# The MLP's second product by seven block products instead of eight, in a two-layer encoder on one core

## The chip, the core and the metric

The kernel runs on one core of a Trainium2 chip. The core has a matrix engine (TensorE, in the profile PE, its weight loads PEld), three engines for elementwise work (VectorE is DVE, ScalarE is ACT, GpSimd is POOL) and SyncE (SP), whose queue issues the loads here. Each engine works through its own list of instructions in order and waits on semaphores for the others. Matrix products read on-chip memory (SBUF) and write into PSUM, of which there are eight banks of 128 x 512 float32. The metric is the device time of one execution in microseconds, as the median of several runs; lower is better.

## The reference

Two layers over 256 tokens of 2048 features, float32. Each layer normalises, projects into three groups of attention heads, sends their outputs through an output projection, and ends in an MLP with 8192 hidden features:

```python
x = x + jnp.einsum('bse,ed->bsd', mix, w_o[l])
h = rmsnorm(x, norm_mlp[l])
u = jax.nn.relu(jnp.einsum('bsd,df->bsf', h, w_up[l]))      # (256, 2048) x (2048, 8192)
x = x + jnp.einsum('bsf,fd->bsd', u * u, w_down[l])          # (256, 8192) x (8192, 2048)
```

A final norm follows the second layer. The two MLP products read 134 MB of weights per layer, each weight once.

## The kernel before

**Three passes for one product.** Every dense product is made in float32 accuracy from a narrower matmul format: an operand a is split into hi (a cast, on ACT) and lo = a - hi (a subtraction, on DVE), and the matmuls hi x hi, hi x lo and lo x hi are added up in PSUM. Activations are split once; each weight tile is split after its load.

**Tiles and steps.** The program is a list of steps, one per weight tile of 128 x 1024 float32 (512 KB): two blocks of 128 rows by 512 columns. For each step `load` (L770) issues the DMA into one of six `wraw` buffers, seven steps ahead; `split` (L776) makes `whi` (L783, ACT) and `wlo` (L784, DVE), two steps ahead, in four buffers each; then the step's `mm` records its matmuls. After each step a queue of background pieces (attention, transposes) may add some PE work; in the MLP there is none. The instructions' order on each engine comes from a scheduler that runs over what the Python code records.

**First product of the MLP** (`up_steps`, L592). Weights are the stationary operand, so features come out on partitions and the 256 tokens on columns. A chunk of 512 features takes two banks and 8 steps of 24 matmuls with 256 columns (L611 to L613). Then for each bank: ReLU on ACT (L617), the square on POOL (L618), hi on ACT (L621), lo on DVE (L622). The norm's factor is left out here, as it passes through ReLU and square as its square.

**Second product** (`down_steps`, L626). For a group g of 1024 hidden features and a chunk j of 512 output columns, 4 steps of 12 matmuls with 512 columns (`mode_b`, L446 to L448) fill two banks, one per block of 128 tokens. DVE then adds each bank, times the squared norm factor, into the residual x (L643). The first product's chunks of group g + 1 are recorded ahead of the second product of group g.

The buffers the change touches: 24 general ones of 4 KB per partition (`big`), 6 of 2 KB (`mid`), six PSUM banks for products and transposes, and two more (`S`) for attention scores.

Of the kernel before, what the change touches and what calls it, by code (L numbers as in the profile page):

```python
# [17 lines left out]
F32 = mybir.dt.float32  # L18
# [5 lines left out]
P = 128  # L24
# [10 lines left out]
# mixer feature blocks of 256 (two k-blocks each): A 0-1, B 2-3, C 4-7  # L35
# [8 lines left out]
def tile_trunk(ctx: ExitStack, tc: tile.TileContext, x_in, w_in, w_o, w_up, w_down,  # L44
# [19 lines left out]
    def big(dt, *shape):  # L64
        return dp.tile([P, *shape], dt, tag="big", bufs=24, name=nm("big"))

    def mid(dt, *shape):
        return dp.tile([P, *shape], dt, tag="mid", bufs=6, name=nm("mid"))
# [4 lines left out]
    def mm_bank():  # L73
        return pp.tile([P, 512], F32, tag="bank", bufs=6, name=nm("mm"))

    def tr_bank():
        return pp.tile([P, 512], F32, tag="bank", bufs=6, name=nm("tr"))

# [10 lines left out]
    ones = cp.tile([P, 64], F32, name="ones")  # L89
# [16 lines left out]
    def setup_tables():  # L106
        """Rope tables with the gains folded in: out = x * ctab + swap16(x) * stab."""
# [14 lines left out]
    def setup_avec():  # L122
        """Relative-position vector of group A, reversed: avec[h, i] = bias(h, rel = 255 - i)."""
# [3 lines left out]
        oh = dp.tile([33, 512], F32, tag="mid", bufs=6, name="oh")  # L127
        nc.sync.dma_start(oh, onehot)
        avs = dp.tile([8, 512], F32, tag="mid", bufs=6, name="avs")
# [30 lines left out]
    def tick():  # L160
        cur[0] += 2.6
# [16 lines left out]
    def hprep(key, gcol, j, hT, ss, done, fin_rs, late=0):  # L178
        """Column chunk j of x: partial sums of squares; k-blocks 4j..4j+3 of the operand."""
# [59 lines left out]
    def q_transposes(src, pr0, qT):  # L239
        """src [P, t, heads*64]; 4 heads from pair pr0 -> qT [hi;lo, 4, 256]."""  # L240
# [13 lines left out]
    def k_transposes(src, pr0, npr, kh, kl):  # L254
        """src [P, t, heads*64]; head pairs pr0.. -> hi/lo [every head in both halves, heads, 256]."""
# [13 lines left out]
    def v_split(ps, parts, t, r):  # L269
        """Value columns of one bank, scaled, as hi/lo; parts: (first column, heads, tile)."""  # L270
# [7 lines left out]
    def rope(raw, H, which, l, outs):  # L278
        """raw [P, t, H, 64]: per-head RMS norm, gain and axial rotary, in place of outs(t)."""
# [29 lines left out]
    def queue_unit(u, *preps):  # L309
        """Scores, transposes of the weights, product with the values; spaced for the softmax between."""  # L310
# [6 lines left out]
    def unit_scores(u):  # L317
        S = pp.tile([P, 4, 256], F32, tag="S", bufs=1, name=nm("S"))
        for s in range(4):
            qh, kh, qb = u.slot(s)  # L320
            st = u.qT[:, qh, qb * P:(qb + 1) * P]
            nc.tensor.matmul(S[:, s, :], st, u.kh[:, kh, :], start=True, stop=False)  # L322
            nc.tensor.matmul(S[:, s, :], st, u.kl[:, kh, :], start=False, stop=True)  # L323
# [4 lines left out]
        if u.kind == "C":  # L328
            nc.vector.tensor_reduce(negm, S, axis=AX.X, op=ALU.max, negate=True)
            src = S  # L330
        else:
            for b in range(2):
                nc.vector.scalar_tensor_tensor(p[:, 2 * b:2 * b + 2, :], S[:, 2 * b:2 * b + 2, :], 0.125,
# [7 lines left out]
            src = p  # L341
# [601 lines left out]
```

## Time and profile before

| | |
|---|---|
| runs | median 2088.99 us of 3 (2088.61 to 2090.86) |
| profiled execution | span 2088.3 us from its first to its last instruction; granted TensorE clock 0.997 on the mean |
| instructions | 31322 |
| loads | 381.49 MB, 183 GB/s on the mean |

The three runs lie within 0.1% of each other, and the span of the profiled execution is 0.7 us below their median. The page gives busy times of each engine, the chain of work that ended last, and groups of instructions by line. In a group's row, the two numbers behind the first bar are its busy time in us and the mean of one instruction in ns; behind the second bar stands how long the engine was idle just ahead of them and what ended that. `128x1024 f32` is partitions by elements. In a timeline's row the first number is the start and the second the duration, both in us. In a table of stretches each engine has its busy time and, in brackets, its instructions, in the order PE, PEld, DVE, ACT, POOL; then come the granted clock (1.00 is full), the busy share of the DMA queues and GB/s. Matmuls overlap each other in PE's pipeline, so the mean of one (0.389 us for 512 columns) is longer than the distance from one to the next.

### The profile page before, as it was taken

What the parts mean: (1) busy time and instruction counts of PE and PEld (TensorE: products, weight loads), DVE (VectorE), ACT (ScalarE), POOL (GpSimd) and SP (SyncE); (2) the same over time, 40 slices, a digit from 0 to 9 for tenths busy, and PEclk for the clock granted to TensorE, in tenths of its full rate; (3) what the DMA queues carried; (4) which work ended last, traced back from release to release, by engine and by line L of the source; (5) the groups of instructions that cost most, each with busy time, mean ns of one, the idle gap of its engine ahead of it and who ended that gap; (6) DMA issues with size and microseconds to landing.
All of it is one profiled execution on the core that took longest, in us unless ns stands there. A gap on an engine that the chain in (4) does not pass through costs nothing.

```text
span 2088.3 us, 31322 instructions
## 1 busy us (share of the span) xinstructions
PE 2066.0 (99%) x12444; PEld 1847.9 (88%) x12444; DVE 1273.8 (61%) x1426; ACT 1041.4 (50%) x1472; POOL 340.1 (16%) x362
## 2 busy tenths in 40 slices
PE   9999999999999999999999999999999999999998
PEld 7878889989899898998888788899899898999986
DVE  6777976454555545555668789754555545555555
ACT  6657755444344444434556566554344444434444
POOL 0484420000000000000005844101000000000001
PEclk9999999999999999999999999999999999999999
DMA  8545455565655656556556453555655656565563
GB/s 289 179 160 157 155 185 176 183 192 180 194 186 187 192 183 192 187 188 189 188 177 188 141 170 130 180 174 181 194 188 183 192 189 191 184 192 185 190 212 121
DMA packets 107550, 381.49 MB, mean 183 GB/s; under 512 B 11875, under 2 KB 14691, under 8 KB 107404
## 3 DMA queue, kind: packets, MB, share of 16 engines
q1 hardware_dynamic: 107116, 378.45, 56.6%
q8 instruction: 97, 1.59, 0.3%
q10 hardware_dynamic: 288, 1.05, 0.1%
q14 instruction: 49, 0.40, 0.1%
HBM read 377.34 MB, written 2.11 MB: 182 GB/s over the span
## 4 chain that ended last, share of the span: by engine, by line
PE 94%; POOL 2%; DVE 1%; ACT 1%; issue 1%; DMA 0%; SPq 0%; POOLq 0%; DVEq 0%
PE mm L446 18%; PE mm L447 18%; PE mm L448 18%; PE mm L612 12%; PE mm L613 12%; PE mm L611 12%; PE tr L362 1%; PE tr L192 1%; PE tr L381 1%; PE S L323 1%; PE S L322 1%; POOL big L300 1%; POOL big L506 0%; PE tr L245 0%; POOL sm L235 0%
## 5 line engine op out<-in xcount | busy, mean ns | idle before, releaser
L784 DVE TENSOR_TENSOR wlo<-wraw,whi 128x1024 fp32r<-128x1024 f32 (+1 forms) x697 | 863.4, 1241 | 697.4 <-ACT whi L783 695.0
L783 ACT CAST whi<-wraw 128x1024 fp32r<-128x1024 f32 (+1 forms) x697 | 729.9, 1048 | 884.6 <-PE mm L448 473.0
L446 PE MATMUL mm<-whi,big 128*128 128x512 f32 (+1 forms) x1792 | 695.7, 389 | 3.1 <-DVE big L252 3.1
L447 PE MATMUL mm<-wlo,big 128*128 128x512 f32 (+1 forms) x1792 | 693.0, 387 | 0.0
L448 PE MATMUL mm<-whi,big 128*128 128x512 f32 (+1 forms) x1792 | 692.4, 386 | 0.0
L611 PE MATMUL mm<-big,whi 128*128 128x256 f32 x2048 | 579.8, 283 | 0.0
L613 PE MATMUL mm<-big,wlo 128*128 128x256 f32 x2048 | 579.6, 283 | 0.0
L612 PE MATMUL mm<-big,whi 128*128 128x256 f32 x2048 | 579.6, 283 | 0.0
L446 PEld LDWEIGHTS mm<-whi,big 128*128 128x128 f32 x1792 | 337.8, 189 | 68.1 <-issue 3.4
L448 PEld LDWEIGHTS mm<-whi,big 128*128 128x128 f32 x1792 | 337.4, 188 | 68.0
L447 PEld LDWEIGHTS mm<-wlo,big 128*128 128x128 f32 x1792 | 337.9, 189 | 64.8 <-DVE wlo L784 0.2
L612 PEld LDWEIGHTS mm<-big,whi 128*128 128x128 f32 x2048 | 393.2, 192 | 0.5
L611 PEld LDWEIGHTS mm<-big,whi 128*128 128x128 f32 x2048 | 393.1, 192 | 0.5
L613 PEld LDWEIGHTS mm<-big,wlo 128*128 128x128 f32 x2048 | 393.1, 192 | 0.0
L618 POOL TENSOR_TENSOR mid<-mid 128x512 f32<-128x512 f32 x64 | 74.2, 1159 | 1247.3 <-ACT mid L617 1247.3
L353 POOL TENSOR_SCALAR big<-big,sm 128x256 f32<-128x256 f32 x128 | 87.5, 701 | 230.3 <-DVE sm L351 164.3
L643 DVE SCALAR_TENSOR_TENSOR x<-mm,sm,x 128x512 f32<-128x512 f32 x128 | 89.9, 744 | 4.5 <-PE mm L448 4.5
L622 DVE TENSOR_TENSOR big<-mid,big 128x512 fp32r<-128x512 f32 x64 | 44.1, 689 | 50.7 <-ACT big L621 50.7
L621 ACT CAST big<-mid 128x512 fp32r<-128x512 f32 x64 | 39.8, 621 | 50.7 <-POOL mid L618 50.7
L617 ACT ACTIVATE mid<-mm,zero 128x512 f32<-128x512 f32 x64 | 43.8, 684 | 39.5 <-PE mm L613 39.5
L235 POOL TENSOR_TENSOR sm<-sm,mhalf 128x2 f32<-128x2 f32 (+3 forms) x16 | 24.7, 1547 | 131.0 <-DVE sm L230 117.0
L364 DVE TENSOR_TENSOR big<-tr,big 128x512 fp32r<-128x512 f32 x64 | 41.1, 680 | 0.3
(117 smaller groups left out, 1013.2 us busy)
## 6 DMA issues: line engine op xcount, KB each, us to landing
wraw<-in_w_up_dram SPq DMA_DIRECT2D x256, 512.0 KB, 4.3
wraw<-in_w_down_dram SPq DMA_DIRECT2D x256, 512.0 KB, 4.1
wraw<-in_w_in_dram SPq DMA_DIRECT2D x120, 512.0 KB, 3.3
wraw<-in_w_o_dram SPq DMA_DIRECT2D x64, 512.0 KB, 3.6
biasB<-in_rpb_dram SPq DMA_DIRECT2D x16, 349.5 KB, 6.2
biasA<-avec SPq DMA_DIRECT2D x4, 768.0 KB, 4.9
x<-in_x_dram SPq DMA_DIRECT2D x3, 512.0 KB, 9.1
big<-in_gfin_dram SPq DMA_DIRECT2D x2, 512.0 KB, 4.3
```

Source lines behind the costliest of these rows:

```text
L353: nc.gpsimd.tensor_scalar(p[:, s, :], p[:, s, :], rs[:, s:s + 1], 1.0, op0=ALU.mult, op1=ALU.mult)
L446: nc.tensor.matmul(o, a_h, wh[:, i, :], start=first and i == 0, stop=False)
L447: nc.tensor.matmul(o, a_h, wl[:, i, :], start=False, stop=False)
L448: nc.tensor.matmul(o, a_l, wh[:, i, :], start=False, stop=last and i == len(sub) - 1)
L611: nc.tensor.matmul(o, sh, ht[:, 0, kk, :], start=s0, stop=False, skip_group_check=True)
L612: nc.tensor.matmul(o, sh, ht[:, 1, kk, :], start=False, stop=False, skip_group_check=True)
L613: nc.tensor.matmul(o, sl, ht[:, 0, kk, :], start=False, stop=s1, skip_group_check=True)
L618: nc.gpsimd.tensor_mul(a, a, a)
L622: nc.vector.tensor_sub(uf[:, 1, :], a, f(uf[:, 0, :]))
L643: nc.vector.scalar_tensor_tensor(xs, box["b"][t], st["r2"][:, t:t + 1], xs, op0=ALU.mult, op1=ALU.add)
L783: last_hi[0] = nc.scalar.copy(h[:, part], w[:, part]).ins
L784: nc.vector.tensor_sub(lo[:, part], w[:, part], f(h[:, part]))
```

## The change

**Seven products.** The second product is cut into quads: 1024 hidden features by 1024 output columns (group g, half n). In a quad, tokens are halved (two blocks of 128), output columns are halved (two of 512), and the features of each step are two blocks of 128. That is a 2 x 2 by 2 x 2 block product, and the Winograd form of Strassen's algorithm makes it with 7 products of sums instead of 8 products. The sums of activation blocks and of weight blocks are made on POOL, the hi/lo split is made of the sums, and the 7 products are summed over the quad's 4 steps in 7 banks. At its end the banks are combined into the four blocks of x, by ACT, DVE and POOL (`down_evac`). The last half of the last group (g = 7, n = 1) stays a plain product (`down_last`, 8 steps of 12 matmuls).

**Activations.** The first product is made in units of 256 features with one bank: 4 steps of 24 matmuls with 256 columns. Since sums of two token blocks need the tokens' factors in them, the squared norm factor now goes into the activations: a row of 256 factors is laid out over all partitions once per layer (`st["rr"]`, made with two matmuls), and POOL multiplies by it. `F` holds eight blocks of 128 columns: the four of the unit and four sums.

**Weights.** A quad step has two tiles, ra and rb. POOL makes four differences of 512 columns (`forms`, one of them in place in ra); what is split then are ra, rb and three half tiles in `T`: 7 blocks of 512 columns for 4. `whi` and `wlo` share ten buffers, of which a quad step takes eight.

**Order.** A pair of quad steps and a unit of the first product follow each other: in each group 0 to 6, pair, unit, four times over, the two quads of the group one after the other. The last quad's four steps stand together.

**Else.** Attention scores take two banks of a common set of eight. `big` has 22 buffers, `mid` 7.

```diff
+        def up_unit(q):
...
+                    for kk in range(4):
+                        ht, hk = st["hT2"][2 * k + kk // 2], kk % 2
+                        for fs in range(2):
+                            o = box["b"][:, fs * 256:(fs + 1) * 256]
...
+                    if k == 3:
+                        up_evac(q, box["b"])
+                return Step([w_up[l, q * 4 + k]], 4, 256, pre, mm, 2.9)
+        def up_evac(q, bank):
+            need(("rr", l))
+            a = mid(F32, 512)
+            nc.scalar.activation(a, bank, AF.Relu, bias=zero1[:, 0:1])
+            nc.scalar.activation(a, a, AF.Square, bias=zero1[:, 0:1])
+            F = big(F32, 8, P)
+            av = a.rearrange("p (k t c) -> p t k c", k=2, t=2)
+            rv = st["rr"].rearrange("p (t o c) -> p t o c", t=2, o=1)
+            for t in range(NT):
+                s0 = 2 - 2 * t
+                nc.gpsimd.tensor_mul(F[:, s0:s0 + 2, :], av[:, t], rv[:, t].to_broadcast([P, 2, P]))
+            nc.gpsimd.tensor_add(F[:, 4, :], F[:, 0, :], F[:, 1, :])
+            nc.gpsimd.tensor_sub(F[:, 5, :], F[:, 2, :], F[:, 0, :])
+            nc.gpsimd.tensor_sub(F[:, 6, :], F[:, 4, :], F[:, 2, :])
+            nc.gpsimd.tensor_sub(F[:, 7, :], F[:, 3, :], F[:, 6, :])
+            c0 = 0 if q >= 28 else 1
+            Fh, Fl = big(F32R, 8, P), big(F32R, 8, P)
+            nc.scalar.copy(Fh[:, c0:8, :], F[:, c0:8, :])
+            nc.vector.tensor_sub(Fl[:, c0:8, :], F[:, c0:8, :], f(Fh[:, c0:8, :]))
+            uT[q] = (Fh, Fl)
+        PRODUCTS = ((2, 0, 0), (4, 2, 0), (3, 1, 1), (7, 1, 0), (6, 2, 1), (5, 0, 1), (1, 3, 0))
+        def down_quads(g, n):
...
+                    Fh, Fl = uT[4 * g + p]
+                    for o, (a, part, i) in zip(box["b"], PRODUCTS):
+                        bh, bl = w[part][0][:, i, :], w[part][1][:, i, :]
+                        nc.tensor.matmul(o, Fh[:, a, :], bh, start=p == 0, stop=False)
+                        nc.tensor.matmul(o, Fh[:, a, :], bl, start=False, stop=False)
+                        nc.tensor.matmul(o, Fl[:, a, :], bh, start=False, stop=p == 3)
+                    if p == 3:
+                        down_evac(n, box["b"])
...
+        def down_evac(n, banks):
...
+            nc.scalar.copy(s1, p1)
+            nc.scalar.copy(s5, p5)
+            nc.vector.tensor_add(x11, x11, p2)
+            nc.vector.tensor_add(x12, x12, p3)
+            nc.vector.tensor_add(u2, s1, p6)
+            nc.vector.tensor_add(u3, u2, p7)
+            nc.vector.tensor_sub(x21, x21, p4)
+            nc.gpsimd.tensor_add(x11, x11, s1)
+            nc.gpsimd.tensor_add(col2, col2, one(s5))
+            nc.gpsimd.tensor_add(x12, x12, u2)
+            nc.gpsimd.tensor_add(row1, row1, one(u3))
...
+        steps.extend(alternate(up_unit(0), up_unit(1)) + up_unit(2) + up_unit(3))
         for g in range(8):
-            if g < 7:
-                up_steps(g + 1)
-            down_steps(g)
+            down = down_quads(g, 0) + (down_quads(g, 1) if g < 7 else down_last(1))
+            per = len(down) // 4
+            for i in range(4):
+                if g == 7:
+                    steps.extend(down[:4] if i == 0 else down[4:] if i == 1 else [])
+                    continue
+                steps.extend(down[per * i:per * i + per])
+                steps.extend(up_unit(4 * (g + 1) + i))
...
+    def part(w, first=False):
+        k, n = w.shape[1:]
+        h = wp.tile([P, k, n], F32R, tag="whl", bufs=10, name=nm("whi"))
+        lo = wp.tile([P, k, n], F32R, tag="whl", bufs=10, name=nm("wlo"))
...
+        if s.forms:
+            ra, rb = raw
+            T = sp.tile([P, 3, 512], F32, tag="bias", bufs=2, name=nm("forms"))
+            nc.gpsimd.tensor_sub(T[:, 0, :], ra[:, 1, :], ra[:, 0, :])
+            nc.gpsimd.tensor_sub(ra[:, 1, :], rb[:, 0, :], ra[:, 1, :])
+            nc.gpsimd.tensor_sub(T[:, 1, :], rb[:, 0, :], T[:, 0, :])
+            nc.gpsimd.tensor_sub(T[:, 2, :], T[:, 1, :], rb[:, 1, :])
+            parts_t[i] = [part(ra), part(rb), part(T[:, 0:2, :]), part(T[:, 2:3, :])]
+            return
```

What the change does to the lists of POOL and ACT shows best in their order. POOL before, at the seam from attention to the MLP (L408 to L417 are the last sums of squares of attention, L618 the squares of the first product; from there on the list holds only L618 to the layer's end):

```order
L408 TENSOR_TENSOR mid_595_2993<-mid_578_2900 128x512
L417 TENSOR_TENSOR sqacc_557_2795<-sqacc_557_2795,mid_595_2993 128x256 x2
L235 TENSOR_TENSOR sm_609_3058<-sm_608_3056,mhalf_83 128x2
L618 TENSOR_TENSOR mid_698_3584<-mid_698_3584 128x512
L618 TENSOR_TENSOR mid_700_3590<-mid_700_3590 128x512
```

POOL in the change, for one pair and its operand: the forms of the pair's second step (L900 to L903), the operand made of the unit ahead of the pair (L652 to L656), and the start of the next pair's forms with the first addition into x (L706) among them:

```order
L900 TENSOR_TENSOR forms_1084_5601<-wraw_1054_5416 128x512
L901 TENSOR_TENSOR wraw_1054_5416<-wraw_1055_5418,wraw_1054_5416 128x512
L902 TENSOR_TENSOR forms_1084_5601<-wraw_1055_5418,forms_1084_5601 128x512
L903 TENSOR_TENSOR forms_1084_5601<-forms_1084_5601,wraw_1055_5418 128x512
L652 TENSOR_TENSOR big_1079_5586<-mid_1078_5583,rr_693_3397 128x256 x2
L653 TENSOR_TENSOR big_1079_5586<-big_1079_5586 128x128
L654 TENSOR_TENSOR big_1079_5586<-big_1079_5586 128x128
L655 TENSOR_TENSOR big_1079_5586<-big_1079_5586 128x128
L656 TENSOR_TENSOR big_1079_5586<-big_1079_5586 128x128
L900 TENSOR_TENSOR forms_1112_5780<-wraw_1082_5597 128x512
L901 TENSOR_TENSOR wraw_1082_5597<-wraw_1083_5599,wraw_1082_5597 128x512
L706 TENSOR_TENSOR x_78<-x_78,mid_1097_5672 128x512
```

Two instructions per 512 features have become a steady list: eight forms and six operand passes per pair, and four additions into x per quad.

ACT before, where two banks of the first product end (L783 casts of weights, L617 ReLU, L621 the operand's cast):

```order
L783 CAST whi_1030_6004<-wraw_1008_5850 128x1024
L617 ACTIVATE mid_1020_5970<-mm_997_5734,zero1_85 128x512
L783 CAST whi_1033_6022<-wraw_1011_5880 128x1024
L621 CAST big_1021_5973<-mid_1020_5970 128x512
L617 ACTIVATE mid_1022_5976<-mm_998_5735,zero1_85 128x512
L621 CAST big_1023_5979<-mid_1022_5976 128x512
```

ACT in the change, at the end of a unit (the four casts of the pair's first step, then the second step's casts, with ReLU L645, square L646 and the operand's cast L659 among them):

```order
L890 CAST whi_1113_5785<-wraw_1082_5597 128x1024
L890 CAST whi_1115_5789<-wraw_1083_5599 128x1024
L890 CAST whi_1117_5793<-forms_1112_5780 128x1024
L890 CAST whi_1119_5797<-forms_1112_5780 128x512
L890 CAST whi_1128_5848<-wraw_1093_5643 128x1024
L645 ACTIVATE mid_1121_5825<-mm_1104_5693,zero1_85 128x512
L646 ACTIVATE mid_1121_5825<-mid_1121_5825,zero1_85 128x512
L890 CAST whi_1130_5852<-wraw_1094_5645 128x1024
L659 CAST big_1123_5835<-big_1122_5828 128x896
L890 CAST whi_1132_5856<-forms_1127_5843 128x1024
```

The operand's cast, which needs the six POOL passes, stands ahead of the casts of the second step's forms; DVE's subtractions stand in the same order.

More of the change, by code (lines that the diff above doesn't have):

```diff
@@ L158, in emit, with tick @@
         p.fn()
-    def tick():
-        cur[0] += 2.6
+    def tick(us):
+        cur[0] += us
         spent = 0.0
@@ L317, in unit_scores @@
     def unit_scores(u):
-        S = pp.tile([P, 4, 256], F32, tag="S", bufs=1, name=nm("S"))
+        S = [mm_bank().rearrange("p (h c) -> p h c", h=2) for _ in range(2)]
         for s in range(4):
@@ new lines, in down_evac @@
+        def down_evac(n, banks):
+            p1, p5, p2, p3, p6, p7, p4 = banks
+            c = n * 1024
+            x11, x12 = x[:, 0, c:c + 512], x[:, 0, c + 512:c + 1024]
+            x21 = x[:, 1, c:c + 512]
+            row1 = x[:, 1, c:c + 1024].rearrange("p (o d) -> p o d", o=2)
+            col2 = x[:, :, c + 512:c + 1024]
+            s1, s5, u2, u3 = (mid(F32, 512) for _ in range(4))
+            one = lambda v: v.rearrange("p (o d) -> p o d", o=1).to_broadcast([P, 2, 512])
+            nc.scalar.copy(s1, p1)
[9 more added lines that the diff above has]
+            nc.gpsimd.tensor_add(row1, row1, one(u3))
@@ L647, in mm @@
                             final_block(0)
-                            for i, (hts, vh, vl) in enumerate(box["w"]):
-                                mode_b(box["b"], hts, vh, vl, [0, 1], i == 0, i == 3, blocks=(1,))
+                            for i, v in enumerate(box["w"]):
+                                run(v, i, (1,))
                             evac(1)
```

221 lines of the change are left out of this document (126 added, 95 removed).

## The prediction

> **What bounds the kernel now.** I read the page's engine table first, then the chain that ended last.
>
> ```profile
> span 2088.3 us, 31322 instructions
> PE 2066.0 (99%) x12444; PEld 1847.9 (88%) x12444; DVE 1273.8 (61%) x1426; ACT 1041.4 (50%) x1472; POOL 340.1 (16%) x362
> ...
> PE 94%; POOL 2%; DVE 1%; ACT 1%; issue 1%; DMA 0%; SPq 0%; POOLq 0%; DVEq 0%
> ```
>
> TensorE (PE) is busy for 99% of the span and is 94% of the chain, so removed matmuls are worth their full time as long as nothing else becomes later. A busy row doesn't give the pace of a pipelined matmul, so I took that from the timeline of PE inside a second-product stretch, and from a table of two stretches of the MLP.
>
> ```profile
> 700.31 0.39 PE L447 MATMUL mm<-wlo,big 128*128 128x512 f32 x1
> ...
> 707.11 0.39 PE L447 MATMUL mm<-wlo,big 128*128 128x512 f32 x1
> ```
>
> ```profile
> 340.00:380.00 40.00, 40.00 (x336) 40.00 (x335) 18.35 (x17) 18.92 (x22) 4.58 (x4) 1.00 0.57 185
> 700.00:800.00 100.00, 100.00 (x624) 90.71 (x623) 52.82 (x51) 42.45 (x44) 4.64 (x4) 1.00 0.59 190
> ```
>
> Between the two timeline rows lie 30 starts (every third is L447), so a 512-column matmul costs 6.80 / 30 = 0.2267 us. The stretch 340 to 380 holds only the first product's 256-column matmuls: 40 / 336 = 0.119 us each. In the second row (PE, PEld, DVE, ACT, POOL in that order) 100 us of mixed MLP leave DVE at 53, ACT at 42 and POOL at under 5: this room is what the change spends.
>
> **What the change removes.** A quad is 1024 rows by 1024 columns of the second product: before, 8 tiles of 12 matmuls, 96; now 4 steps of 7 products with 3 passes each, 84. That is 12 x 0.2267 = 2.72 us for each of 15 quads in each of two layers (the sixteenth stays plain): **81.6 us**. The first product has the same matmuls in another order: nothing.
>
> **What it adds, for one period.** In steady state a *pair* of quad steps is followed by one unit of the first product; there are 4 pairs in each of 7 groups in 2 layers, 56. PE needs 42 x 0.2267 + 96 x 0.119 = **20.94 us** for a pair and its unit. The other engines' rows, shapes kept apart:
>
> ```profile
> L784 DVE TENSOR_TENSOR wlo<-wraw,whi 128x1024 fp32r<-128x1024 f32 x695 | 862.1, 1242 | 697.4 <-ACT whi L783 695.0
> L783 ACT CAST whi<-wraw 128x1024 fp32r<-128x1024 f32 x695 | 728.8, 1050 | 884.6 <-PE mm L448 473.0 <-PE mm L612 341.8 <-issue 58.2
> ...
> L643 DVE SCALAR_TENSOR_TENSOR x<-mm,sm,x 128x512 f32<-128x512 f32 x128 | 89.9, 744 | 4.5 <-PE mm L448 4.5
> ...
> L618 POOL TENSOR_TENSOR mid<-mid 128x512 f32<-128x512 f32 x64 | 74.2, 1159 | 1247.3 <-ACT mid L617 1247.3
> L622 DVE TENSOR_TENSOR big<-mid,big 128x512 fp32r<-128x512 f32 x64 | 44.1, 689 | 50.7 <-ACT big L621 50.7
> L617 ACT ACTIVATE mid<-mm,zero 128x512 f32<-128x512 f32 x64 | 43.8, 684 | 39.5 <-PE mm L613 39.5
> ```
>
> ACT: 10 casts of 1024 columns, 2 of 512 (about 0.6), one of 896 (about 0.92, between 0.6 and 1.05), two passes over the bank at 0.68, and every second pair two bank copies of about 0.6: 10.5 + 1.2 + 0.9 + 1.4 + 0.6 = 14.6 us of 20.94, hidden. DVE: 10 subtractions of 1024 (1.24), 2 of 512 (0.69), one of 896 (1.10): 14.9, and 5 bank reads (0.74) every second pair, 1.9: 16.8, hidden if it is alone. Loads: the same bytes as before, hidden at 0.59 of the queues.
>
> POOL: 8 subtractions of 512 columns for the weight forms, then for the operand 2 products of 256 and 4 sums of 128, and every second pair the additions into x, 2 of 512 and 2 of 1024. Before it had two passes of 512 for as much of the first product. The rows nearest to these, two separate tensors in SBUF in each:
>
> ```profile
> L290 POOL TENSOR_TENSOR big<-big,sm 128x1024 f32<-128x1024 f32 x4 | 8.1, 2027 | 0.3
> ...
> L493 POOL TENSOR_TENSOR mid<-big,big 128x256 f32<-128x256 f32 x4 | 2.9, 736 | 0.2
> ```
>
> ```profile
> 149.57 1.27 POOL L506 TENSOR_TENSOR big<-big,big 128x512 f32<-128x512 f32 x1
> ```
>
> At 1.27 for 512, 0.74 for 256, 2.03 for 1024 and 0.47 for 128 (on the line through 0.74 and 1.27) a pair costs POOL 10.2 + 1.5 + 1.9 + 3.3 = 16.8 us. Each engine alone would fit. **But they don't run alone.** The timelines of POOL and of DVE in the rope stretch, where POOL has work today:
>
> ```profile
> 119.26 1.30 POOL L296 TENSOR_TENSOR big<-big,ctab_q 128x512 f32<-128x512 f32 x1
> 120.51 2.28 POOL L506 TENSOR_TENSOR big<-big,big 128x512 f32<-128x512 f32 x1
> ```
>
> ```profile
> 120.10 1.55 DVE L784 TENSOR_TENSOR wlo<-wraw,whi 128x1024 fp32r<-128x1024 f32 x1
> ```
>
> ```profile
> 143.38 1.30 POOL L296 TENSOR_TENSOR big<-big,ctab_q 128x512 f32<-128x512 f32 x1
> ```
>
> ```profile
> 143.61 2.15 DVE L784 TENSOR_TENSOR wlo<-wraw,whi 128x1024 fp32r<-128x1024 f32 x1 [1.35 <-ACT whi L783]
> ```
>
> L506 takes 1.27 alone and 2.28 beside a weight subtraction: that one ends at 120.10 + 1.55 = 121.65 and L506 ends 1.14 later, at 122.79. In the other order the subtraction takes 2.15 for 1.24: L296 ends at 144.68 and the subtraction 1.08 later. So one waits until the other has ended, and only the first 0.13 to 0.16 us of each lie beside it. Both are passes over two SBUF operands; so are all that the change adds to POOL, and all of DVE's subtractions. I therefore add their exclusive parts: DVE 10 x 1.08 + 2 x 0.54 + 0.945 = 12.8; POOL (each duration less 0.13) 8 x 1.14 + 2 x 0.61 + 4 x 0.34 + (2 x 1.14 + 2 x 1.90) / 2 = 14.7; together **27.6 us** against PE's 20.94.
>
> The Trainium skill (SBUF — State Buffer, Who interferes with whom) has this as a lock that a two-input VectorE instruction and a GpSimd instruction that reads SBUF hold for the whole instruction. By that wording the full durations add, 14.9 + 16.8 = 31.7 us for a pair, and the sum below would be about 2645; the rows say a little less, and I go by the rows.
>
> To 27.6 comes some idling. When a unit's bank is finished, POOL's operand passes wait for two ACT passes, 2 x 0.684 = 1.4 us, and DVE's later subtractions for casts behind these; behind the six POOL passes ACT's cast of the operand blocks its queue, with the casts of the second quad step's forms behind it, which PE waits for at its fifth matmul of that step. I take 1.4: 29.0, which is 8.03 above PE's need, and 56 x 8.03 = **450 us**.
>
> The last quad of a layer has four steps with no unit between: DVE 4 x (3 x 1.08 + 0.54) = 15.1, POOL 16 x 1.14 = 18.2, together 33.4 against 84 x 0.2267 = 19.0: 14.3, twice **29 us**. The factor row made once per layer, the score banks taken from the common tag and the smaller operand pool lie under PE work of the stage ahead: nothing, at worst a few us.
>
> **Sum.** 2088.3 - 81.6 + 450 + 29 = 2485.7 for the profiled execution; the median of the runs is 0.7 above its span, so **2486 us**, 19% slower. Bounds of the unknown price: if a form costs POOL only what its cheapest row of 512 does (L618 shows 1.04 beside an idle DVE, 0.91 of it exclusive) and the rest 0.8 of mine, 7.3 + 2.1 + 2.4 + 12.8 = 24.6 and no idling: 3.7 x 56 + 21 gives 2235. If nothing overlaps, 31.7 and the idling on top, 12.2 x 56 + 38 gives 2727. I stay near the exclusive parts, since both quoted events agree on them. POOL's spans are rough, which is why I keep both ends.
>
> **Rivals.** *POOL and DVE work side by side after all* (0.16). For it: POOL is only 16% busy now, and the events are few. Then POOL's own queue decides. After a unit 1.4 + 3.4 (six passes) + 0.92 (operand cast) + 1.05 (form cast) = 6.7 us stand against PE's 4.76 + 0.91 to its fifth matmul of the second step: 1.0 x 56. In every second pair two forms, the additions into x and four forms (2.5 + 6.6 + 5.1 = 14.2) stand in POOL's queue ahead of the next operand, against a unit of 11.4: 2.8 x 28. That gives 2088.3 - 81.6 + 57 + 78 + 3, about 2145: slower, but by 3%.
>
> *Faster* (0.10): the forms and the operand are ready ahead of their steps, and only the matmuls count: 2007 to 2080. It decides from a pair of 22.3 us down, since the gain of 81.6 pays for 1.4 us in each of 58 such places. POOL's share would have to fall from 14.7 to about 9 us or be hidden from DVE. Against it: the two events, and six POOL passes in a row between a unit's end and the second quad step.
>
> *The clock falls as well* (inside the forecast). PE had one long wait for a rope product:
>
> ```profile
> 120.00:130.00 10.00, 7.20 (x32) 5.97 (x31) 7.18 (x9) 4.90 (x8) 9.76 (x10) 0.86 0.64 210
> 130.00:140.00 10.00, 10.00 (x49) 8.35 (x49) 7.51 (x10) 5.43 (x7) 4.87 (x5) 0.97 0.23 67
> ```
>
> With PE idle for 2.8 us the granted clock reads 0.86 and then 0.97, a loss of 1.4 + 0.3 = 1.7 us. After each pair's wait that would be up to 95 us more, 2580, if PE and not the other two sets the end by then.
>
> That the products are fewer isn't in doubt: 84 matmuls of 512 stand in the order of each quad.
>
> **How the numbers follow.** Forecast 0.70 (2235 to 2700), side by side 0.16 (2090 to 2235), faster 0.10, above 2700 0.04. Within 0.2%, which is about what a measurement of this kernel can tell from no change, only the seam between the two rivals falls: 0.02, so faster 0.10, same 0.02, slower 0.88. The range 2120 to 2700 leaves out the faster case, the top and the low part of the side-by-side case, 0.2 together.
>
> **What would show it.** Right: in the group table the weight subtraction on DVE well above 1.24 us and the form subtractions on POOL well above 1.27, DVE and POOL together near or over the stretch in any MLP window, PE at 70 to 75% there, waiting for forms' casts and subtractions in the second step of each pair and POOL in the chain. Wrong: durations as in today's rows with both busy at once (then the first rival), or PE still at 99% of the span (then the second). A pair takes 29 us from one unit's end to the next by the forecast, 23 to 25 by the first rival, 21 by the second.

## The result and the profile after

The changed kernel takes **2559.43 us** (median of 4 runs, 2557.30 to 2563.38) against 2089.70 us before (4 runs, 2088.61 to 2090.86): 1.225 times as long, with an interval of 1.223 to 1.227. The forecast was 2486 us in a range from 2120 to 2700.

The page of the changed kernel: the engine table, the granted clock in 40 slices, and the shares of the chain that ended last.

```profile
span 2559.3 us, 33076 instructions
...
PE 2185.6 (85%) x12092; PEld 1877.4 (73%) x12092; DVE 2007.0 (78%) x1718; ACT 1305.6 (51%) x1836; POOL 1724.0 (67%) x1282
...
PEclk9999999898898998898899999998989999999888
...
PE 42%; POOL 32%; issue 8%; DVE 8%; ACT 7%; DMA 2%; POOLq 0%; DVEq 0%; SPq 0%; ACTq 0%
```

PE's matmuls are 352 fewer, and PE no longer ends last: its share of the chain went from 94% to 42%, and POOL has 32% for 2%. DVE is busy 733 us longer than before. The subtractions of form tiles that the change gave it are 120 of 1024 columns and 120 of 512, at 1.24 and 0.69 us only 232 us. The groups of instructions, shapes apart, say where the rest comes from.

```profile
L891 DVE TENSOR_TENSOR wlo<-wraw,whi 128x1024 fp32r<-128x1024 f32 x695 | 1161.4, 1704 | 240.5 <-ACT whi L890 235.5 <-PE tr L385 2.4
L891 DVE TENSOR_TENSOR wlo<-forms,whi 128x1024 fp32r<-128x1024 f32 x120 | 251.8, 2098 | 6.9 <-ACT whi L890 5.8
```

```profile
L902 POOL TENSOR_TENSOR forms<-wraw,forms 128x512 f32<-128x512 f32 x120 | 230.7, 1923 | 0.0
L901 POOL TENSOR_TENSOR wraw<-wraw,wraw 128x512 f32<-128x512 f32 x120 | 229.3, 1911 | 50.3 <-DMA wraw<-in_w_down_dram 24.1 <-DVE wlo L891 15.2 <-DVE big L660 3.1
...
L652 POOL TENSOR_TENSOR big<-mid,rr 128x256 f32<-128x256 f32 x128 | 133.8, 1065 | 181.3 <-ACT mid L646 181.3
```

The same 695 subtractions that took 1242 ns each now take 1704, those of the form tiles 2098; a form on POOL, 1.27 us in the single event of the kernel before, takes 1.9. The instructions are longer though their shapes are the same: a row's "busy" contains the time in which the instruction is held up by the other engine (experiment 3 takes that time away). So the busy shares (78% and 67%) can't be read as each engine's own work.

The timeline of PE gives the length of a period. The rows are first matmuls of pairs of quad steps in layer 1 (the first pair, three in a row, the last quad) and the plain product's first matmul behind the last quad:

```profile
382.61 0.40 PE L677 MATMUL mm<-whi,big 128*128 128x512 f32 x1
...
473.30 0.40 PE L677 MATMUL mm<-whi,big 128*128 128x512 f32 x1
...
500.73 0.40 PE L677 MATMUL mm<-whi,big 128*128 128x512 f32 x1
...
532.76 0.40 PE L677 MATMUL mm<-whi,big 128*128 128x512 f32 x1
...
1217.68 0.40 PE L677 MATMUL mm<-whi,big 128*128 128x512 f32 x1
...
1254.10 0.39 PE L725 MATMUL mm<-whi,big 128*128 128x512 f32 x1
```

From 382.61 to 1217.68 are 28 pairs with their units: 29.82 us each, for PE work of 20.94. They mostly alternate, here 27.4 us (473.30 to 500.73), then 32.0 (500.73 to 532.76), the long one being that in which a quad's seven banks are added into x. In layer 2 the mean is 29.71 (1652.50 to 2484.27). The last quad takes 36.42 us here (1217.68 to 1254.10) and 38.02 in layer 2.

What PE waits for, in the table of waits (us in total, times, longest):

```profile
ACT big L659 <- POOL big L656: 253.6, 64, 10.0
...
PE mm L677 <- ACT whi L890: 210.0, 59, 8.5
...
PE mm L678 <- DVE wlo L891: 110.3, 55, 3.8
```

PE waits for casts of the second step's forms (`whi`, ACT), nearly always at that step's fifth matmul, as forecast; ACT had been waiting, with the operand's cast (L659) at the head of its queue, for POOL's operand passes (L656). This is the chain that the prediction gave its 1.4 us of idling to. The last row is a wait that the prediction did not name: in every long pair PE also waits 2.7 to 3.8 us at the fifth matmul of the first step, for a low part (`wlo`) from DVE.

### The profile page after: what moved, and what is told of

The parts are those of the page before. It is cut to its first block, busy times and chain, and to the rows that moved or that the text cites. A ratio compares the mean times of both kernels' runs of the same rounds, so it can differ in the third digit from the quotient of the medians.

```text
span 2559.3 us, 33076 instructions
## 1 busy us (share of the span) xinstructions
PE 2185.6 (85%) x12092; PEld 1877.4 (73%) x12092; DVE 2007.0 (78%) x1718; ACT 1305.6 (51%) x1836; POOL 1724.0 (67%) x1282
## 4 chain that ended last, share of the span: by engine, by line
PE 42%; POOL 32%; issue 8%; DVE 8%; ACT 7%; DMA 2%; POOLq 0%; DVEq 0%; SPq 0%; ACTq 0%
DVE wlo L891 6%; PE mm L453 5%; PE mm L454 5%; PE mm L452 5%; POOL big L652 5%; PE mm L635 5%; PE mm L634 5%; PE mm L633 5%; POOL forms L902 4%; POOL x L709 3%; POOL x L707 3%; ACT whi L890 3%; PE mm L678 3%; POOL wraw L901 3%; POOL forms L900 3%
## 5 line engine op out<-in xcount | busy, mean ns | idle before, releaser
L891 DVE TENSOR_TENSOR wlo<-wraw,whi 128x1024 fp32r<-128x1024 f32 (+1 forms) x697 | 1162.7, 1701 | 240.5 <-ACT whi L890 235.5
L677 PE MATMUL mm<-whi,big 128*128 128x512 f32 x840 | 382.6, 456 | 210.1 <-ACT whi L890 210.0
L678 PE MATMUL mm<-wlo,big 128*128 128x512 f32 x840 | 398.0, 474 | 110.5 <-DVE wlo L891 110.3
L891 DVE TENSOR_TENSOR wlo<-forms,whi 128x1024 fp32r<-128x1024 f32 x240 | 406.0, 1723 | 17.7 <-ACT whi L890 16.5
L677 PEld LDWEIGHTS mm<-whi,big 128*128 128x128 f32 x840 | 187.3, 223 | 276.7 <-ACT whi L890 235.5
L679 PE MATMUL mm<-whi,big 128*128 128x512 f32 x840 | 383.0, 456 | 0.0
L890 ACT CAST whi<-forms 128x1024 fp32r<-128x1024 f32 x240 | 196.5, 832 | 223.6 <-PE mm L634 215.4
L452 PE MATMUL mm<-whi,big 128*128 128x512 f32 (+1 forms) x768 | 300.4, 392 | 0.0
L453 PE MATMUL mm<-wlo,big 128*128 128x512 f32 (+1 forms) x768 | 295.6, 385 | 0.6 <-DVE wlo L891 0.6
L454 PE MATMUL mm<-whi,big 128*128 128x512 f32 (+1 forms) x768 | 295.0, 384 | 0.0
L900 POOL TENSOR_TENSOR forms<-wraw 128x512 f32<-128x512 f32 x120 | 206.3, 1719 | 120.3 <-DMA wraw<-in_w_down_dram 74.1
L901 POOL TENSOR_TENSOR wraw<-wraw,wraw 128x512 f32<-128x512 f32 x120 | 229.3, 1911 | 50.3 <-DMA wraw<-in_w_down_dram 24.1
L652 POOL TENSOR_TENSOR big<-mid,rr 128x256 f32<-128x256 f32 x128 | 133.8, 1065 | 181.3 <-ACT mid L646 181.3
L660 DVE TENSOR_TENSOR big<-big,big 128x896 fp32r<-128x896 f32 (+1 forms) x64 | 78.0, 1219 | 208.9 <-ACT big L659 208.9
```

Source lines behind the costliest of these rows:

```text
L452: nc.tensor.matmul(o, a_h, wh[:, i, :], start=first and i == 0, stop=False)
L453: nc.tensor.matmul(o, a_h, wl[:, i, :], start=False, stop=False)
L454: nc.tensor.matmul(o, a_l, wh[:, i, :], start=False, stop=last and i == len(sub) - 1)
L677: nc.tensor.matmul(o, Fh[:, a, :], bh, start=p == 0, stop=False)
L678: nc.tensor.matmul(o, Fh[:, a, :], bl, start=False, stop=False)
L679: nc.tensor.matmul(o, Fl[:, a, :], bh, start=False, stop=p == 3)
```

## The experiments

Two things had to be told apart: how much of the loss is that DVE and POOL hold each other up (theory 1), and how much is the order of the queues, the operand's cast on ACT above all, or something else in the new operations (the rivals). The kernel before took 2090 to 2091.5 us beside each of these runs. Experiments 1 to 9 are one run each and have no interval; the kernels that were run several times spread by 0.1 to 0.4%, and every difference of times read here is above 1%. "Pair" is the mean distance of pairs in layer 1, read as above.

**1. Without POOL's weight differences.**

```diff
-            nc.gpsimd.tensor_sub(T[:, 0, :], ra[:, 1, :], ra[:, 0, :])
...
-            parts_t[i] = [part(ra), part(rb), part(T[:, 0:2, :]), part(T[:, 2:3, :])]
+            parts_t[i] = [part(ra), part(rb), part(ra), part(rb[:, 0:1, :])]
```

> POOL's four weight differences per quad step are left out; the steps split ra, rb, ra again and half of rb, so ACT, DVE and PE do as much as in the change, and the products are not those of the algorithm. Theory 1 (DVE's subtractions and POOL's passes exclude each other, so their sum sets the pair): per pair 12.8 us of DVE and 5.6 us of POOL, 18.4, fall below PE's 20.94; with a us or two of the operand's chain left, pairs at 21.5 to 23 us against 29.8 now, the last quads at PE's 19 to 21 us, and 2559 - 56 x 7.5 - 2 x 17 = about 2105 us. The weight subtractions on DVE back to about 1.3 us in the mean of the MLP. Theory 2 (ACT's queue is held by the operand's cast, which waits for six POOL passes; the shared time on DVE and POOL is a side effect): the cast still stands ahead of the second step's casts, most of its 254 us of waiting stays, about 2300 us.

Measured: 2329.29 us. 230 us of the loss go with 480 POOL passes, but 240 stay although DVE and POOL together are now far from full: the sum of exclusive parts alone (2105) misses, the queue's figure (2300) is near. Two of this kernel's waits, then PE's timeline at the second step of one pair:

```profile
ACT big L659 <- POOL big L656: 194.5, 64, 3.5
...
PE mm L677 <- ACT whi L890: 167.2, 58, 3.0
```

```profile
642.24 0.39 PE L679 MATMUL mm<-whi,big 128*128 128x512 f32 x1
642.47 0.39 PE L677 MATMUL mm<-whi,big 128*128 128x512 f32 x1
645.72 0.79 PE L677 MATMUL mm<-whi,big 128*128 128x512 f32 x1 [2.87 <-ACT whi L890]
646.31 0.63 PE L678 MATMUL mm<-wlo,big 128*128 128x512 f32 x1
646.74 0.63 PE L679 MATMUL mm<-whi,big 128*128 128x512 f32 x1
...
651.43 0.59 PE L679 MATMUL mm<-whi,big 128*128 128x512 f32 x1
651.86 0.39 PE L677 MATMUL mm<-whi,big 128*128 128x512 f32 x1
```

```profile
648.00:650.00 2.00, 2.00 (x6) 1.59 (x5) 1.38 (x2) 1.04 (x1) 0.00 (x0) 0.50 0.92 326
...
652.00:654.00 2.00, 2.00 (x17) 1.88 (x16) 1.94 (x3) 1.68 (x2) 0.00 (x0) 1.00 0.97 373
```

Once in nearly every pair (58 times) PE waits 2.9 us for a cast that stands behind the operand's. Ahead of the wait a matmul follows another after 0.23 us (642.24, 642.47), behind it after 0.43 (646.31, 646.74), until 651.86: the granted clock, the number after the five engines in a stretch's row, is 0.50 (648 to 650) and then 1.00 again. 6.14 us of work at half speed are 2.9 us lost, so this wait cost twice its length. A pair takes 26.15 us on the mean, where the fastest ones of experiment 3 take 21.06: 56 x 5.1 = 285 of the 320.8 us that lie between this span, 2327.5, and the 2006.7 to which only the matmuls' count leads.

**2. The low parts made but not read.**

```diff
-        return h, lo
+        return h, h
```

> The lo part of every weight tile is still subtracted on DVE and written, but the matmuls read the hi part in its place (the result is less exact), so PE no longer waits for DVE's weight subtractions. All engines have the work of the change. Theory 1: the pair's sum of DVE and POOL stays 27.6 us, 2400 to 2540 us, weight subtractions at 1.6 to 1.7 us and form differences at 1.7 to 1.9 us. Theory 2: without the waits of PE for DVE, 2559 - 130 = about 2430 us; the two don't differ here, the run is the partner of the next one.

Measured: 2640.24 us, slower than the whole change and outside what either side expected. It isn't a clean undoing: with no matmul reading `lo`, its buffer comes free when DVE is done and not when PE is, and the lists of ACT and DVE come out in another order. ACT then waited for DVE 740.9 us and POOL's first difference for loads 407.3 us (74.1 in the changed kernel). It shows nothing on its own, and stands as the partner of the next.

**3. DVE's subtraction of two SBUF operands replaced by a sum of one.** As 2, and for the subtraction `whi` is not read: a reduction over the same columns.

```diff
-            nc.vector.tensor_sub(lo[:, c], w[:, c], f(h[:, c]))
-        return h, lo
+            nc.vector.tensor_reduce(f(lo)[:, c, 0], w[:, c], axis=AX.X, op=ALU.add)
+        return h, h
```

> As the run with the lo part unread, but DVE's subtraction of each weight tile is replaced by a sum over the same 1024 (or 512) columns of the raw tile: an instruction as long (1.2 us by the rows of before) that reads one SBUF operand, not two. The lo part is not made. Theory 1: POOL's passes no longer meet a second reader but for the operand's own subtraction; form differences back to about 1.3 us, the sums on DVE at 1.2 us though DVE and POOL are busy at once, pairs at 21.5 to 24 us, 2130 to 2230 us. If the two engines slowed each other by being busy, whatever they read, or if the order of the queues set the pair, it takes as long as its partner within 2%.

Measured: 2214.08 us, 426 us below its partner, with as many DVE instructions. The groups of the partner (2), then of this kernel (3):

```profile
L891 DVE TENSOR_TENSOR wlo<-wraw,whi 128x1024 fp32r<-128x1024 f32 x695 | 1145.9, 1664 | 276.3 <-ACT whi L890 216.4 <-PE mm L454 24.4 <-ACT big L251 9.0
...
L902 POOL TENSOR_TENSOR forms<-wraw,forms 128x512 f32<-128x512 f32 x120 | 252.5, 2104 | 0.0
```

```profile
L891 DVE TENSOR_REDUCE wlo<-wraw 128x2 f32<-128x1024 f32 x431 | 517.3, 1214 | 88.0 <-PE mm L454 68.7 <-PE mm L727 4.5 <-DMA wraw<-in_w_in_dram 3.4
...
L902 POOL TENSOR_TENSOR forms<-wraw,forms 128x512 f32<-128x512 f32 x120 | 155.1, 1293 | 0.0
```

The DVE instruction is as long as the subtraction is alone (1214 against 1242 ns before), so DVE's load is the same, but now POOL's form takes 1293 ns for 2104, and both engines are busy at once (376 and 434 of the 600 us from 400 to 1000). So it is the kind of DVE's instruction, and not DVE's or POOL's amount of work, that makes them exclude each other.

The reduction differs from the subtraction in two ways, though: it has one SBUF input for two, and it writes only two numbers per partition. This kernel's own timeline tells the two apart, for DVE's list still holds the operand's subtraction (L660, two SBUF operands) and additions of a bank to a block of x (L702, one SBUF operand and one PSUM bank), and both write whole rows. Of DVE and of POOL:

```profile
401.68 1.20 DVE L660 TENSOR_TENSOR big<-big,big 128x896 fp32r<-128x896 f32 x1 [4.93 <-ACT big L659]
...
405.65 0.67 DVE L702 TENSOR_TENSOR x<-x,mm 128x512 f32<-128x512 f32 x1
```

```profile
402.01 2.03 POOL L901 TENSOR_TENSOR wraw<-wraw,wraw 128x512 f32<-128x512 f32 x1
...
405.87 1.30 POOL L706 TENSOR_TENSOR x<-x,mid 128x512 f32<-128x512 f32 x1 [0.58 <-DVE x L701]
```

POOL's difference that starts beside L660 takes 2.03 us and ends 1.16 us after it (404.04 for 402.88). From 400 to 1040 us every second L901 meets L660 and takes 2.01 to 2.18; the others take 1.28 to 1.30. POOL's addition beside L702 takes its 1.30 as well. So the second SBUF operand on DVE is what excludes, not how much DVE writes. The Trainium skill (SBUF — State Buffer, Who interferes with whom) says that an instruction with two SBUF inputs contends with GpSimd's reads and that `tensor_reduce` never does on this chip; these rows agree with both.

This kernel is also close to the first rival of the prediction, the engines side by side, but for PE's waits for low parts, which it doesn't have. The rival forecast 23 to 25 us per pair; measured are 24.2.

**4. The operand's cast and subtraction three steps later**, behind the second step's casts in ACT's and DVE's lists. Nothing is left out.

```diff
+            def operand():
+                Fh, Fl = big(F32R, 8, P), big(F32R, 8, P)
+                with nullcontext() if q < 4 else tc.issue_after(last_hi[0]):
+                    nc.scalar.copy(Fh[:, c0:8, :], F[:, c0:8, :])
...
+                later.append((now[0] + 3, operand))
```

> The operand's cast and subtraction are moved behind the casts of the second quad step of the pair and of two tiles of the next unit (from the fifth unit on); nothing else changes, and the result is that of the change. The next reader of the operand comes two pairs later at the earliest. Theory 1: the port's sum of 27.6 us per pair stays, only the idle 1.4 us and some of the short waits go: 2559 - 56 x (0.5 to 2.2) = 2435 to 2530 us. Theory 2: the 254 us that ACT waits with its cast for POOL's passes leave the path: about 2300 us.

Measured: 2480.72 us, 79 us less. One row of stretches of this kernel, from 400 to 1000 us, and two of its groups:

```profile
400.00:1000.00 600.00, 501.99 (x2967) 435.00 (x2966) 543.16 (x331) 295.95 (x340) 588.36 (x338) 0.94 0.44 150
```

```profile
L910 POOL TENSOR_TENSOR forms<-wraw,forms 128x512 f32<-128x512 f32 x120 | 237.3, 1978 | 0.0
...
L899 DVE TENSOR_TENSOR wlo<-wraw,whi 128x1024 fp32r<-128x1024 f32 x695 | 1204.5, 1759 | 241.4 <-ACT whi L898 233.3 <-PE tr L195 1.4 <-PE tr L386 1.2
```

With ACT's wait for POOL's operand passes down to 106.9 us (253.6 in the change), POOL is busy for 98% of the stretch (588.36 of 600) and DVE for 91%, each holding the other's instructions up (1978 and 1759 ns). A pair takes 28.30 us (379.20 to 1171.55 over 28). That is the sum of the exclusive parts, forecast at 27.6, with 0.7 on top; and the 1.4 to 1.5 us that went are as much as the prediction had for idling.

**5. Both: no weight differences, and the operand later.**

> POOL's four weight differences per step are left out (the 7 blocks are split from copies of ra and rb, so the output is not the reference's), and the operand's cast and subtraction are recorded three steps later, behind the casts of the pair's second step. Theory 1, the exclusive parts of DVE and POOL plus ACT's queue held by the operand's cast: per pair 12.8 + 5.6 = 18.4 us are under PE's 20.94, and the 2.87 us for which PE waited in every pair when only the differences were left out (2329.29 us) go: 2020 to 2120, granted clock at 0.98 or above. Rival, the lower granted clock belongs to the seven products themselves and not to the waits: the clock stays near 0.94 and the time at 2200 or above.

Measured: 2203.79 us, 125 us below experiment 1, clock 0.976. The rival falls (the clock rises with the waits gone), but 2020 to 2120 is missed too. The pairs show where the rest lies; three first matmuls in a row:

```profile
595.58 0.40 PE L685 MATMUL mm<-whi,big 128*128 128x512 f32 x1
...
622.12 0.40 PE L685 MATMUL mm<-whi,big 128*128 128x512 f32 x1
...
643.71 0.40 PE L685 MATMUL mm<-whi,big 128*128 128x512 f32 x1
```

Pairs with additions into x take 26.5 us (595.58 to 622.12), those without 21.6 (622.12 to 643.71). In the long one, DVE's subtractions and POOL's additions stand side by side, and PE waits 2.28 us for a low part, after which its matmuls are at half pace until 618.48:

```profile
610.66 3.22 POOL L717 TENSOR_TENSOR x<-x,mid 128x1024 f32<-128x1024 f32 x1
```

```profile
615.02 0.46 PE L636 MATMUL mm<-big,wlo 128*128 128x256 f32 x1 [2.28 <-DVE wlo L899]
```

L717 takes 2.41 us where DVE reads one SBUF operand (the same addition, L709, in experiment 3).

**6. As 5, and without POOL's four additions into x at a quad's end.**

```diff
-            nc.gpsimd.tensor_add(x11, x11, s1)
-            nc.gpsimd.tensor_add(col2, col2, one(s5))
-            nc.gpsimd.tensor_add(x12, x12, u2)
-            nc.gpsimd.tensor_add(row1, row1, one(u3))
```

> Beside what the kernel of 2203.79 us leaves out (POOL's weight differences, with the operand three steps later), POOL's four additions into x at a quad's end are left out as well, so x lacks these terms. In that kernel every second pair, the one with these additions, took 26.5 us and the others 21.6. Theory 1, the additions delay DVE's subtractions beside them and PE then waits at a lowered clock: all pairs take 21 to 21.6, 28 x 5 = 140 us less, 2040 to 2075, below the kernel before. Rival, the pairs with additions are long for DVE's bank reads or ACT's bank copies, which stay: 2170 to 2204.

Measured: 2063.64 us, 140 us less and now below the kernel before; every pair but the first of a layer takes 21.6 us (21.75 and 21.78 on the mean of the layers).

```profile
400.00:1000.00 600.00, 593.86 (x3827) 536.37 (x3826) 446.41 (x430) 386.75 (x445) 165.91 (x168) 1.00 0.55 193
```

PE is busy for 99% at full clock, as before the change. So the seven products do save time, and what eats it is POOL's work beside DVE's: the additions into x cost 140 us (30 quads, 4.7 us each) though POOL was only at 46% in that kernel from 400 to 1000 us.

**7. The weight differences on DVE** (from experiment 4, `nc.gpsimd.tensor_sub` of the four forms becomes `nc.vector.tensor_sub`). Nothing is left out.

> The operand's cast and subtraction three steps later, and the four weight differences made by DVE in place of POOL; nothing is left out. Theory 1, exclusive parts: DVE does the differences in about 0.69 us each, so the two together need 12.8 + 8 x 0.54 + 5.6 = 22.8 us per pair and DVE alone 16.8 + 8 x 0.69 = 22.3; with 1 to 2 us of waits a pair takes 24 to 25: 2170 to 2270 us. Rival, the two engines do not exclude each other and the differences cost because POOL's queue is long: POOL's queue is short now and DVE's 22.3 us alone decide with no additions to them on POOL stretched: 2090 to 2160. Rival, the waits of the loads for free buffers decide: no change from 2480.

Measured: 2264.26 us, 295 us below the change, pair 24.78 us (378.30 to 1072.18). The same passes over the same operands cost less on DVE, 0.68 to 0.75 us on the mean for 1.27 and more on POOL, though there too they hold POOL up (its operand passes of 256 columns take 1.28 us on the mean, 0.74 in experiment 3).

**8. As 7, without the additions into x.**

> The kernel with the weight differences on DVE and the operand three steps later (2264.26 us), without POOL's four additions into x. Theory 1, the sum of exclusive parts falls by (2 x 1.14 + 2 x 1.90) / 2 = 3.0 to 19.8 us per pair, DVE's own 22.3 are left: pairs of 22.3 to 23, 2100 to 2150, still not below the kernel before. Rival, the price of the additions is not in DVE's delays: 2230 to 2264.

Measured: 2126.09 us, pair 22.5 us (22.3 to 22.6 without the first), which is DVE's own sum of 22.3.

```profile
400.00:1000.00 600.00, 584.80 (x3702) 517.07 (x3701) 577.74 (x628) 370.83 (x431) 176.23 (x162) 1.00 0.57 188
```

DVE is at 96% (577.74 of 600) and the clock at 1.00. Even with the additions free, DVE would set the end above the kernel before.

**9. The work shared out: half of the differences and most additions on DVE.** From experiment 4; nothing is left out.

```diff
-            nc.gpsimd.tensor_sub(T[:, 0, :], ra[:, 1, :], ra[:, 0, :])
+            nc.vector.tensor_sub(T[:, 0, :], ra[:, 1, :], ra[:, 0, :])
...
-            nc.gpsimd.tensor_sub(T[:, 1, :], rb[:, 0, :], T[:, 0, :])
+            nc.vector.tensor_sub(T[:, 1, :], rb[:, 0, :], T[:, 0, :])
...
+            nc.vector.tensor_add(x11, x11, p1)
+            nc.vector.tensor_add(x12, x12, p5)
+            nc.vector.tensor_add(x22, x22, p5)
...
-            nc.gpsimd.tensor_add(x11, x11, s1)
-            nc.gpsimd.tensor_add(col2, col2, one(s5))
```

> The operand three steps later, two of the four differences per step on DVE, and most additions into x on DVE straight from the PSUM banks; nothing is left out. Theory 1, exclusive parts: DVE about 12.8 + 4 x 0.54 = 15 us and POOL 4 x 1.14 + 2.6 + 1.5 = 8.7 us, together 23.7 per pair, DVE alone 20.7: pairs of 24 to 25.5 us and 2170 to 2290 us, not below the kernel before. Rival, side by side: PE's 20.94 and DVE's 20.7 decide, 2010 to 2090.

Measured: 2368.75 us, above what was expected and 104 us slower than 7; pair 26.76 for a sum of 23.7. POOL's first difference overwrites a block that DVE's first one reads, and its second one uses the result of DVE's second, so each step hands over twice, and POOL waits:

```profile
POOL wraw L910 <- DVE forms L909: 267.7, 55, 6.4
```

That these waits make the 3 us isn't shown: the additions into x were moved in the same run, and DVE is at 94% there (564.88 of the 600 us from 400 to 1000).

**10. The kernel before with the change's side edits only**: scores from a common set of eight banks, 22 general buffers for 24, 7 of the small ones for 6.

```diff
-        return pp.tile([P, 512], F32, tag="bank", bufs=6, name=nm("mm"))
+        return pp.tile([P, 512], F32, tag="bank", bufs=8, name=nm("mm"))
...
-        S = pp.tile([P, 4, 256], F32, tag="S", bufs=1, name=nm("S"))
+        S = [mm_bank().rearrange("p (h c) -> p h c", h=2) for _ in range(2)]
```

> The kernel before with only the change's side edits: scores from the common set of eight banks, 22 general buffers for 24, 7 of the 2 KB ones for 6. If the 6.4 us by which the first layer's first MLP matmul came later in the changed kernel (334.26 against 327.90) and the like in the second layer come from these edits: 10 to 20 us over before, 2100 to 2110. If they come from the change's own work at the seam (the factor row, the first units): within 3 us of before.

Measured: 2098.31 us (5 runs, 2096.47 to 2103.85), 1.0045 times the time before, interval 1.003 to 1.006. It lies between the two figures: the side edits alone cost 0.45%, in the profiled execution 7.9 us (2096.2 for 2088.3). Of these, 4.6 us lie ahead of the first MLP matmul of layer 1 (332.50 for 327.90).

## Why the prediction was right, and where it was short

**The mechanism held.** The removal of matmuls agrees with what was said: in experiment 6 PE is again at 99% and the kernel 26 us faster than before, although its pairs keep 46 us above 20.94 (28 x 0.81 + 28 x 0.84, for which no run gives a cause), which leaves 9 us of the 81.6 for the last quads and the seams. The exclusion of DVE and POOL, read from two events in the rope stretch, holds over the whole MLP: experiment 3 takes away the second SBUF operand and nothing of DVE's time, and the rows go back to their length but where the one two-operand subtraction that is left meets them; experiment 4 takes away the queue, and what is left is the sum of the exclusive parts to 0.7 us. By the full durations, which the Trainium skill's wording (SBUF — State Buffer, Who interferes with whom) gave, a pair would be 31.7; the 28.30 of experiment 4 is nearer to the rows' 27.6.

**The idling** (1.4 us per pair, 78 us in all) is what experiment 4 took away: 79 us, by moving the cause that was named, ACT's cast of the operand at the head of its queue. That the size fits so closely is in part luck: the 1.4 was the length of the two ACT passes ahead of POOL's, which experiment 4 leaves in place, and the run doesn't split the 79 us over POOL's waits for these passes (181.3 us before it, 123.8 with it) and ACT's for POOL's (253.6 and 106.9). "Side by side" falls with the rows above, and "faster" needed a pair of 22.3 us, which only experiment 6 went below.

**Three terms were too small**, together about 77 us, of which 73.6 are left between the spans (2559.3 for 2485.7):

| term | forecast | measured |
|---|---|---|
| matmuls removed | -81.6 | -81.6 taken as it stands |
| 56 pairs | 450 | 28 x (29.82 - 20.94) + 28 x (29.71 - 20.94) = 494 |
| two last quads | 29 | (36.42 - 19.04) + (38.02 - 19.04) = 36.4 |
| the plain product behind them, in each layer | 0 | 8.0 + 6.5 = 14.5 |
| ahead of each layer's MLP | 0 | 6.4 + 5.0 = 11.4 |
| sum | 397 | 475, for 471 between the spans; the 4 aren't told apart |

*Pairs, 44 us.* 0.7 of the 0.8 us per pair is the sum of the exclusive parts itself, as experiment 4 shows. Most of it is POOL's passes, which were priced too low. In experiment 3 a pass of 512 columns that isn't held takes 1.29 to 1.30 us (forecast 1.27) and an addition of 1024 columns this:

```profile
L707 POOL TENSOR_TENSOR x<-x,mid 128x1024 f32<-128x1024 f32 x30 | 72.3, 2411 | 0.0
```

The forecast had 2.03, from a product (L290) whose second operand is a small factor spread over the columns. Over a pair that is 8 x 0.025 + 0.03 + 0.38, about 0.6 us more, as an estimate. The rest isn't told apart.

*Behind and between the MLPs, 26 us: "nothing, at worst a few us" failed.* The first MLP matmul of layer 1 starts at 334.26 for 327.90. These rows of before and after are the first and the last matmul of the second product's last half in layer 1 (after, the first is the one at 1254.10 above), and the first of layer 2's MLP:

```profile
1024.91 0.39 PE L446 MATMUL mm<-whi,big 128*128 128x512 f32 x1
...
1048.23 0.39 PE L448 MATMUL mm<-whi,big 128*128 128x512 f32 x1
...
1361.93 0.36 PE L611 MATMUL mm<-big,whi 128*128 128x256 f32 x1
```

```profile
1259.07 0.33 PE L194 MATMUL tr<-ident,x 128*128 128x128 f32 x1 [1.87 <-POOL x L708]
1262.35 3.04 PE L194 MATMUL tr<-ident,x 128*128 128x128 f32 x13 [2.95 <-POOL x L709]
...
1285.43 0.39 PE L727 MATMUL mm<-whi,big 128*128 128x512 f32 x1
...
1604.15 0.36 PE L633 MATMUL mm<-big,whi 128*128 128x256 f32 x1
```

The half, plain in both kernels, takes 31.3 us for 23.3 (in layer 2 28.0 for 21.5, 2522.29 to 2550.30 for 2058.06 to 2079.59). In layer 1 the transposes of the next layer stand in it and wait 1.87 and 2.95 us for POOL's last additions into x, with the clock at 0.50 from 1260 to 1265; before, DVE finished x bank by bank beside PE's matmuls. From the last MLP matmul of layer 1 to the first of layer 2 it is 318.7 us for 313.7. Of the 6.4 and 5.0 us ahead of the MLPs, experiment 10 puts 4.6 and 3.3 on the side edits (332.50 for 327.90, and 1052.84 to 1369.81, 317.0 us, for 313.7). The prediction costed `down_evac` only inside the pairs and asked nowhere who reads x after the last one.

**"The clock falls as well"** was put inside the forecast as up to 95 us. It does fall (0.90 on the mean from 400 to 1000 us, where PE is busy for 82% and not the 70 to 75% that were to show the forecast right), and experiment 1 shows its full price where PE sets the end. In the changed kernel itself its share can't be read off, since in experiment 4, at 0.94, POOL is full and the clock costs little; that stays open.

**No version that leaves nothing out beats the kernel before.** The best of them is experiment 7, 2264 us. Its sum of exclusive parts is 22.8 us per pair and DVE's own 22.3; moving work back to POOL raises the sum (1.14 for a form that costs DVE 0.54), and the break-even of 22.3 us per pair was worked out without the 26 us that lie outside the pairs and the last quads.

## What to carry to other kernels

Before giving an idle engine work, look in the trace for a stretch where it already works beside its neighbour, and compare the same instruction's duration there and alone; here DVE passes over two SBUF operands and POOL passes over SBUF added up nearly as if they ran on one engine (28.3 us per pair in experiment 4, 27.6 by their exclusive parts), and the busy shares of both hid it, for each counts the time that it is held. Follow every new wait down the queue of the engine in between: here a cast that waited for POOL held up casts that had their data, and 79 us came back by recording it three steps later. A step that is added at a stage's end has a reader in the next stage, which belongs in the sum.

## What the runs showed that was not expected

A wait of PE of 2.87 us halves the granted clock, and it stayed there for 6 us of work (experiment 1), so that such a wait in each period costs up to double; the prediction's event, with 0.86 and 0.97 in stretches of 10 us, had hidden this depth in its mean. The Trainium skill (TensorE: Matmul & The Clock Gate, What's actually happening) gives about 3.4 us of idling for the fall and as much busy time for the return; here less idling was enough (2.28 us in the pair of experiment 5 that is shown, with 3.5 us at half pace behind it), and the return took up to 6.1 us.

Leaving a value unread made a kernel slower (experiment 2, 81 us above the change): what reads a buffer also sets when it comes free, and the order of the other engines' lists came out differently with it. Which of the two cost the time isn't told apart.
